# A mixture of 32 experts in plain float32, by quarters of 32 slots on column tiles, with 20 weight tiles in flight, in a fused diffusion block

## The chip, the cores and the metric

One core of one Trainium2 chip runs the whole block as one program. TensorE (PE) multiplies matrices, VectorE (DVE) and ScalarE (ACT) work elementwise, GpSimd (POOL) issues the indirect transfers, SyncE (SP) issues most of the others, and 16 DMA engines move the data between the chip's memory and the core. The metric is the device time of one execution in microseconds (us); smaller is better.

## The reference

A token-mixing sub-layer (a state-space branch and a convolution branch) comes first and isn't touched by the change. The second sub-layer is a mixture of experts over 512 tokens of 1024 channels: each token goes to 2 of 32 experts, and each expert is a SwiGLU with a hidden width of 256. A last normalisation follows.

```python
def hier_moe(h, w_rg, b_rg, w_rx, b_rx, w_gate, w_up, w_down):
    ...
    expert_id = g_idx * EXPERTS_PER_GROUP + top_idx
    gate = jnp.sum(jax.nn.one_hot(expert_id, N_EXPERTS, dtype=jnp.float32) * weights[..., None], axis=1)
    gate = gate.astype(h.dtype)
    out = jnp.zeros_like(h)
    for e in range(N_EXPERTS):
        act = jax.nn.silu(h @ w_gate[e]) * (h @ w_up[e])
        out = out + gate[:, e:e + 1] * (act @ w_down[e])
    return out
...
            x = x + gt2 * out.reshape(x.shape)
...
    return rmsnorm(x, g_final)
```

One expert has three matrices of 256 Ki float32 numbers, 1 MB each; all 32 have 96 such matrices, 100.7 MB. With the inputs of this case, 20 experts have at most 32 tokens, 8 have 33 to 64, 2 have 65 to 96 and 2 have more (up to 128); so cut into quarters of 32 slots, the 32 experts fill 20 + 16 + 6 + 8 = 50 quarters. The last expert fills one.

## The kernel before

The span up to about 550 us is the token mixing, the routing and its tables. Then comes the expert loop, iterations `e` = 0 to 32, with the instruction order of PE, ACT and DVE written out by hand (`tc.manual_schedule`), and a last part that adds everything up.

**Slots.** Each expert has 128 slots. `gather_e` fetches the rows of an expert's tokens into one of two buffers `xg` by an indirect transfer (line 1325), two iterations ahead. `tile_x` transposes them on PE (line 1337, eight 128x128 transposes) into `st`, as a rounded high part and a low remainder, since the matmuls run in the faster but coarser format float32r.

**Weights.** They arrive as thirds of an expert, 1 MB each, in 13 tiles that `eraw` hands out in turn: two thirds hold half of gate and up each, one holds down. `load_p(m)` issues third `m` on SP's queue. ACT and DVE split every third into a high and a low part (`unit_hi` line 1297, `unit_lo` line 1302, `unit_d_hi`, `unit_d_lo` lines 1312 and 1316).

**Products.** `tile_gu` makes 24 matmuls of 128x512 per expert (lines 1349 to 1351: high by high, low by high, high by low), always over all 128 slots; `tile_act` applies SwiGLU, `tile_at` transposes the result (line 1362), `tile_down` makes 12 matmuls (lines 1372 to 1375), `tile_y` copies them to `y` on ACT, and `scatter_e` writes the rows used with one indirect transfer to `ybuf` in memory (line 1329); branches on POOL alone choose its size. The results of the last two experts (`DIRECT`) don't go through memory: `last_y` splits them and `last_out` multiplies them with a one-hot matrix.

**Last part.** `last_loads` brings the residual stream `x1` (2 MB, twice 1 MB) and the last scale `gfin`, `last_rows` reads each token's two rows of `ybuf`. `last_add0` and `last_add1` weigh and add them on ACT, DVE and POOL, `last_out` adds the matmuls of the last two experts, squares and takes the root, `last_norm` scales and writes each block of 128 tokens out.

PE's order in an iteration is: half of gate and up of `e`, transposes of the activations of `e-1`, transposes of `x` for `e+1`, down of `e-1`, second half of gate and up of `e`.

Of the kernel before, what the change touches and what calls it, by code (L numbers as in the profile page):

```python
# [26 lines left out]
def hybrid_kernel(  # L27
# [952 lines left out]

    def eraw(name):
# [8 lines left out]
        if j < 11:  # L990
            return modp.tile([128, 2048], F32, tag=("ch", "cl")[j - 9], name=name)
        if j == 11:
            er2[0] = xp.tile([128, 4096], F32, tag="x16", name=name)
        return er2[0][:, 2048 * (j - 11):2048 * (j - 11) + 2048]

    def part_load(gate, up, down, h, q=SY):

        t = eraw("eraw")
        if h < 2:
            t = t.rearrange("p (a k n) -> p a k n", a=2, k=4)  # L1000
            for a, src in enumerate((gate, up)):
                q.dma_start(out=t[:, a], in_=src[512 * h:512 * h + 512].rearrange("(p k) n -> p k n", k=4))
        else:
            t = t.rearrange("p (k n) -> p k n", k=2)
            q.dma_start(out=t, in_=down.rearrange("(p k) n -> p k n", k=2))
        return t
# [3 lines left out]
    def load_p(m, *a):  # L1010
        if m < 3 * 32:
            e = m // 3
            eraws.setdefault(e, []).append(part_load(w_exp_gate[0, e], w_exp_up[0, e], w_exp_down[0, e], m % 3, *a))
# [211 lines left out]
    for m in range(7, 9):  # L1225
        load_p(m)
    NXG = 2
    gt2 = mo.tile([128, D], F32, name="gt2", tag="gt2", bufs=1)
    SY.dma_start(out=gt2, in_=adr[6:8].rearrange("(o n) d -> o (n d)", o=1).to_broadcast([128, D]))
    xgs = [mo.tile([128, D], F32, name=f"xg{j}", tag=f"xg{j}", bufs=1) for j in range(NXG)]  # L1230
# [18 lines left out]
    def indices(pt, p, n, name):  # L1249
# [10 lines left out]
        V.tensor_tensor(ix[:, 0], em[:, 0], em[:, 1], op=ALU.add)  # L1260
        return ix

    pt = ps_tp("ptab")
# [26 lines left out]
    def gu_views(r, q, u):  # L1290
        src = r[q // 2][:, :, 2 * (q % 2):2 * (q % 2) + 2, :].rearrange("p a k n -> p k a n")
        return [t.rearrange("p k (a n) -> p k a n", a=2) for t in u] + [src]
# [7 lines left out]
    def unit_lo(r, q, u, keep=False):  # L1300
        hi, lo, src = gu_views(r, q, u)
        i = V.tensor_tensor(lo, src, hi.bitcast(F32), op=ALU.subtract)  # L1302
        if keep:
            tc.keep_in_program_order(i)
        return u

    def unit_gu(r, q):
        return unit_lo(r, q, unit_hi(r, q))

    def unit_d_hi(r, q):  # L1310
        u = [mo.tile([128, 1024], F32R, tag=t, name="e" + t, bufs=2) for t in ("dh", "dl")]
        S.activation(u[0], r[2][:, q, :], AF.Copy)  # L1312
        return u

    def unit_d_lo(r, q, u, keep=False):
        i = V.tensor_tensor(u[1], r[2][:, q, :], u[0].bitcast(F32), op=ALU.subtract)  # L1316
        if keep:
            tc.keep_in_program_order(i)
        return u

    def unit_d(r, q):
        return unit_d_lo(r, q, unit_d_hi(r, q))

# [8 lines left out]
    def tile_x(xg, st, h):  # L1332

        pt = ps_tp("pxt").rearrange("p (k s) -> p k s", k=4)
        for k in range(4):

            T.transpose(pt[:, k, :], xg[:, 512 * h + k:512 * h + 512:4], ident)  # L1337
        sh_ = st[:, 4 * h:4 * h + 4]
        S.activation(sh_[:, :, 0, :], pt, AF.Copy)  # L1339
        V.tensor_tensor(sh_[:, :, 1, :], pt, sh_.bitcast(F32)[:, :, 0, :], op=ALU.subtract)  # L1340

    def new_st():
        return mo.tile([128, KD, 2, 128], F32R, tag="st", name="st")

    def tile_gu(pg, st, unit, q):
        w_h, w_l = unit
        for k2 in range(2):
            k = 2 * q + k2
            T.matmul(pg, lhsT=st[:, k, 0, :], rhs=w_h[:, k2, :], start=(k == 0), stop=False)  # L1349
            T.matmul(pg, lhsT=st[:, k, 1, :], rhs=w_h[:, k2, :], start=False, stop=False)  # L1350
            T.matmul(pg, lhsT=st[:, k, 0, :], rhs=w_l[:, k2, :], start=False, stop=(k == KD - 1))  # L1351

    def tile_act(pg):
        sg = mo.tile([128, 256], F32, tag="sge", name="sge", bufs=1)
        S.activation(sg, pg[:, 0:256], AF.Silu)
        V.tensor_tensor(sg, pg[:, 256:512], sg, op=ALU.mult)
        return sg

    def tile_at(sg):
        pa = ps_s5("pat")[:, 0:256].rearrange("p (k s) -> p k s", k=2)  # L1360
        for k in range(2):
            T.transpose(pa[:, k, :], sg[:, k:256:2], ident)
        at = mo.tile([128, 2, 2, 128], F32R, tag="at", name="at", bufs=1)
        S.activation(at[:, :, 0, :], pa, AF.Copy)  # L1364
        V.tensor_tensor(at[:, :, 1, :], pa, at.bitcast(F32)[:, :, 0, :], op=ALU.subtract)
        return at

    def tile_down(pd, at, unit, k):
        w_h, w_l = unit
# [336 lines left out]
```

## Time and profile before

| what | value |
|---|---|
| median of 3 runs | 911.4 us (910.17 to 912.75) |
| profiled execution, its own time | 909.51 us |
| span of the profiled execution | 907.8 us |
| mean granted clock of TensorE | 0.943 |
| PE busy | 778.0 us (86%) |
| DVE busy | 677.7 us (75%) |
| ACT busy | 543.7 us (60%) |
| POOL busy | 375.9 us (41%) |
| mean DMA rate over the span | 224 GB/s |

Busy times overlap, so they don't add up. The span is what the profiler recorded from the first to the last instruction; 1.7 us lie around it in the execution's own time. Busy shares are means over stages that have different limits; the windows of the trace tell them apart.

### The profile page before, as it was taken

The numbers are of one execution on the slowest core, as the hardware profiler recorded it, in microseconds if no ns is written. First come the engines' busy times: TensorE is split into PE (matmuls) and PEld (weight loads), VectorE is DVE, ScalarE is ACT, GpSimd is POOL, SyncE is SP. The second block draws the span as 40 slices with busy tenths as digits, with TensorE's granted clock in tenths as the row PEclk, the third lists the DMA queues.
The fourth block names the chain that finished last, engine by engine and source line by source line (L and its number), as shares of the span: only waits on it lengthen the run. The fifth ranks groups of instructions, "written<-read, shape, count | busy, mean of one in ns | idle before, by whom it ended". The sixth has DMA issues, their size and how long they took to land.

```text
span 907.8 us, 14079 instructions
## 1 busy us (share of the span) xinstructions
PE 778.0 (86%) x5094; PEld 602.4 (66%) x5094; DVE 677.7 (75%) x914; ACT 543.7 (60%) x839; POOL 375.9 (41%) x291
## 2 busy tenths in 40 slices
PE   3598957988878977979999976999999999999972
PEld 0376845656556765736788755788888888888751
DVE  4948473473599778637874596999999999999867
ACT  4433512435365756538432435989888898898752
POOL 4657434534477696712400221233323332333443
PEclk9988987999989998989999987999999999999976
DMA  8925951232146464468857346989999998988222
GB/s 307 254 66 168 224 188 53 72 122 71 39 143 192 132 183 162 142 233 310 287 205 296 116 184 228 393 336 340 365 367 372 375 387 327 354 307 307 80 118 92
DMA packets 89988, 201.88 MB, mean 222 GB/s; under 512 B 12558, under 2 KB 42320, under 8 KB 85810
## 3 DMA queue, kind: packets, MB, share of 16 engines
q1 hardware_dynamic: 82658, 180.00, 56.5%
q0 software_dynamic: 4832, 12.44, 3.9%
q10 hardware_dynamic: 2416, 8.44, 3.5%
q8 instruction: 40, 0.66, 0.3%
q14 instruction: 42, 0.34, 0.1%
HBM read 180.16 MB, written 22.76 MB: 224 GB/s over the span
## 4 chain that ended last, share of the span: by engine, by line
PE 53%; DVE 14%; issue 9%; DMA 9%; POOL 8%; ACT 4%; SPq 3%; ACTq 0%; POOLq 0%; DVEq 0%
PE peg L1351 6%; PE peg L1349 6%; PE peg L1350 6%; DMA wa<-in_w_ada_dram 4%; PE cp L804 3%; PE ped L1372 3%; PE pxt L1337 3%; PE ped L1373 3%; PE ped L1375 3%; POOL adacc L98 2%; PE po L1192 2%; PE po L1191 2%; PE po L1190 2%; DVE so L681 1%; DVE st L95 1%
## 5 line engine op out<-in xcount | busy, mean ns | idle before, releaser
L1302 DVE TENSOR_TENSOR ewwl<-eraw,ewwh 128x1024 fp32r<-128x1024 f32 x96 | 120.2, 1253 | 7.3 <-PE pxt L1337 4.0
L1297 ACT ACTIVATE ewwh<-eraw 128x1024 fp32r<-128x1024 f32 x96 | 101.9, 1063 | 5.8 <-DMA eraw<-in_w_exp_gate_dram 3.6
L1325 POOL DMA_INDIRECT xg<-h2d,tb x32 | 49.1, 1536 | 110.9 <-PE ped L1372 87.2
L1329 POOL DMA_INDIRECT ybuf<-ye,tb x30 | 42.6, 1421 | 94.0 <-ACT ye L1380 92.9
L1316 DVE TENSOR_TENSOR edl<-eraw,edh 128x1024 fp32r<-128x1024 f32 x64 | 75.5, 1221 | 5.8 <-ACT edh L1312 5.7
L396 PE MATMUL zp<-hh,zuwh 128*128 128x512 f32 x192 | 78.1, 407 | 0.0
L1349 PE MATMUL peg<-ewwh,st 128*128 128x512 f32 x192 | 77.4, 403 | 0.0
L1350 PE MATMUL peg<-ewwh,st 128*128 128x512 f32 x192 | 77.0, 401 | 0.0
L1351 PE MATMUL peg<-ewwl,st 128*128 128x512 f32 x192 | 76.7, 400 | 0.0
L398 PE MATMUL zp<-hh,zuwl 128*128 128x512 f32 x192 | 76.3, 398 | 0.4 <-POOL zuwl L752 0.2
L397 PE MATMUL zp<-hl,zuwh 128*128 128x512 f32 x192 | 75.9, 395 | 0.0
L1312 ACT ACTIVATE edh<-eraw 128x1024 fp32r<-128x1024 f32 x64 | 67.8, 1060 | 10.2 <-PE ped L1375 10.1
L98 POOL TENSOR_TENSOR adacc<-adacc,wa 128x512 f32<-128x512 f32 x30 | 46.2, 1540 | 41.4 <-ACT wa L854 39.0
L1372 PE MATMUL ped<-edh,at 128*128 128x512 f32 x128 | 53.2, 416 | 1.2 <-ACT at L1364 1.2
L1373 PE MATMUL ped<-edl,at 128*128 128x512 f32 x128 | 50.2, 392 | 0.0
L808 ACT ACTIVATE cpt<-cp 128x512 f32<-128x512 f32 x16 | 8.3, 602 | 61.3 <-PE cp L804 49.7
L396 PEld LDWEIGHTS zp<-hh,zuwh 128*128 128x128 f32 x192 | 36.9, 192 | 11.6 <-issue 4.4
L398 PEld LDWEIGHTS zp<-hh,zuwl 128*128 128x128 f32 x192 | 36.6, 191 | 9.5 <-POOL zuwl L752 1.6
L1351 PEld LDWEIGHTS peg<-ewwl,st 128*128 128x128 f32 x192 | 36.7, 191 | 9.1
L1350 PEld LDWEIGHTS peg<-ewwh,st 128*128 128x128 f32 x192 | 36.4, 190 | 8.9 <-DVE st L1340 0.4
L1349 PEld LDWEIGHTS peg<-ewwh,st 128*128 128x128 f32 x192 | 36.5, 190 | 8.6 <-ACT st L1339 0.3
L397 PEld LDWEIGHTS zp<-hl,zuwh 128*128 128x128 f32 x192 | 36.8, 192 | 7.2
(491 smaller groups left out, 2207.7 us busy)
## 6 DMA issues: line engine op xcount, KB each, us to landing
eraw<-in_w_exp_down_dram SPq DMA_DIRECT2D x31, 1024.0 KB
eraw<-in_w_exp_gate_dram SPq DMA_DIRECT2D x61, 512.0 KB
eraw<-in_w_exp_up_dram SPq DMA_DIRECT2D x61, 512.0 KB
wa<-in_w_ada_dram SPq DMA_DIRECT2D x32, 512.0 KB
zr<-in_w_in_dram SPq DMA_DIRECT2D x12, 1024.0 KB
wa<-in_w_ada_dram SPq DMA_DIRECT2D x8, 1024.0 KB
ybuf<-zero ACTq DMA_DIRECT2D x4, 1024.0 KB
gd<-sg SPq DMA_DIRECT2D x16, 256.0 KB
```

What stands on the lines that cost most here:

```text
L396: T.matmul(acc, lhsT=wh, rhs=ah, start=start, stop=False)
L397: T.matmul(acc, lhsT=wh, rhs=al, start=False, stop=False)
L398: T.matmul(acc, lhsT=wl, rhs=ah, start=False, stop=stop)
L1297: S.activation(hi, src, AF.Copy)
L1302: i = V.tensor_tensor(lo, src, hi.bitcast(F32), op=ALU.subtract)
L1312: S.activation(u[0], r[2][:, q, :], AF.Copy)
L1316: i = V.tensor_tensor(u[1], r[2][:, q, :], u[0].bitcast(F32), op=ALU.subtract)
L1349: T.matmul(pg, lhsT=st[:, k, 0, :], rhs=w_h[:, k2, :], start=(k == 0), stop=False)
L1350: T.matmul(pg, lhsT=st[:, k, 1, :], rhs=w_h[:, k2, :], start=False, stop=False)
L1351: T.matmul(pg, lhsT=st[:, k, 0, :], rhs=w_l[:, k2, :], start=False, stop=(k == KD - 1))
L1372: T.matmul(pd[h], lhsT=at[:, k, 0, :], rhs=w_h[:, hs[h]], start=(k == 0), stop=False)
L1373: T.matmul(pd[h], lhsT=at[:, k, 0, :], rhs=w_l[:, hs[h]], start=False, stop=False)
```

## The change

Six edits come together.

1. The split into high and low parts is gone, with its ACT and DVE instructions. Weights and slots stay plain float32, and so do the matmuls.
2. Each expert's 128 slots are cut into quarters `a` of 32. `tile_gu` and `tile_down` run per quarter: the 32 slots are the stationary operand, on one of four 32-column tiles of the array (the output's partitions `Q[c]`), and the four tiles take four parts of the output's columns. `quarters` wraps quarters 1 to 3 in nested branches on the expert's size, on PE (for the matmuls) and on POOL (for the scatters); `load_wide` reads the size into a PE register. `scatter_q` writes one quarter by one indirect transfer in pieces of 256 numbers (1 KB), since the output's four column parts now lie on different partitions.
3. Weights in flight: `NER` = 20 thirds instead of 13. A third is now one whole matrix (gate, up or down), 8 KB on each partition. Three more tiles come from `mo`, four more thirds from pairs of tiles of `wp` (`PIECES`) that were used for the split weights of the token mixing. The order of the ring changes with it: thirds 7 to 12 are issued when the token mixing's pool is closed, 13 to 16 on ACT's queue, 17 and 18 on SP's, the others at the end of each iteration.
4. `tile_y` moves from ACT to DVE and multiplies by the sub-layer's gate `gt2q` there, which the last part did before.
5. Tables of the scatter get four quarters (`ixq`, 16 small matmuls and one DVE instruction, once).
6. The last part adds in PSUM: `last_x` puts the residual into PSUM accumulators `fin` by an identity matmul, `last_own` adds the last two experts, `last_mix` adds the weighed rows by an identity matmul, `last_sum` squares, `last_root` and `last_norm` finish. POOL takes no part in it any more.

The core of the diff:

```diff
-        j = erc[0] % 13
+        while erc[0] % NER in PIECES:
+            erc[0] += 1
+        j = erc[0] % NER
...
-    def unit_hi(r, q):
-        u = wpair(q, [2, 512], "ew")
-        hi, lo, src = gu_views(r, q, u)
-        S.activation(hi, src, AF.Copy)
-        return u
...
-            T.matmul(pg, lhsT=st[:, k, 0, :], rhs=w_h[:, k2, :], start=(k == 0), stop=False)
-            T.matmul(pg, lhsT=st[:, k, 1, :], rhs=w_h[:, k2, :], start=False, stop=False)
-            T.matmul(pg, lhsT=st[:, k, 0, :], rhs=w_l[:, k2, :], start=False, stop=(k == KD - 1))
+    def tile_gu(pg, st, r, a):
+        for k in range(KD):
+            for c in range(4):
+                src = r[c // 2][k // 4][:, 256 * (k % 4) + c % 2:256 * (k % 4) + 256:2]
+                T.matmul(pg[Q[c], 128 * a:128 * a + 128], lhsT=st[:, k, Q[a]], rhs=src, start=(k == 0), stop=(k == KD - 1), skip_group_check=True)
...
+    def tile_down(pd, at, r, a):
         for k in range(2):
+            for c in range(4):
+                T.matmul(pd[a // 2][Q[c], 256 * (a % 2):256 * (a % 2) + 256], lhsT=at[:, 64 * a + 32 * k:64 * a + 32 * k + 32], rhs=r[2][k][:, 256 * c:256 * c + 256],
+                         start=(k == 0), stop=(k == 1), skip_group_check=True)
...
+    def scatter_q(e, a, y):
+        return G.indirect_dma_start(out=ybuf.rearrange("r (c n) -> (r c) n", c=4), out_offset=bass.IndirectOffsetOnAxis(ap=ixq[:, a, e:e + 1], axis=0),
+                                    in_=y[:, 256 * a:256 * a + 256], in_offset=None, bounds_check=8 * L - 1, oob_is_err=False)
+
+    def quarters(size_, f):
+
+        r = [f(0)]
+        with tc.If(size_ > SIZES.index(32)):
+            r.append(f(1))
+            with tc.If(size_ > SIZES.index(64)):
+                r.append(f(2))
+                with tc.If(size_ > SIZES.index(96)):
+                    r.append(f(3))
+        return r
...
+        for a in range(4):
+            for c in range(4):
+                V.tensor_tensor(y[Q[a], 256 * c:256 * c + 256], pd[a // 2][Q[c], 256 * (a % 2):256 * (a % 2) + 256], gt2q[Q[c]], op=ALU.mult)
...
+    def last_mix(i):
         y = yrs[i][:, 0]
+        S.activation(y, y, AF.Copy, scale=pw[:, i, 0:1])
         V.scalar_tensor_tensor(y, yrs[i][:, 1], pw[:, i, 1:2], y, op0=ALU.mult, op1=ALU.add)
...
+        for h in range(2):
+            T.matmul(fin[i][h], lhsT=ident, rhs=y[:, 512 * h:512 * h + 512], start=False, stop=True, skip_group_check=True)
...
+                quarters(wide[e], lambda a: tile_gu(pgs[e % 2], st[e], eraws[e], a))
+            load_wide(e + 1)
+            if e == NE:
+                last_x(0)
             if e > 0:
                 at = tile_at(sg)
+            if e == NE:
+                fin[1], fin[2] = pgs, [ps_tp(f"fin2{i}") for i in range(2)]
+                last_x(1)
+                last_x(2)
...
+                quarters(wide[e - 1], lambda a: tile_down(pd, at, eraws[e - 1], a))
...
+            for m in range(3 * e + 19, 3 * e + 22):
+                load_p(m)
```

How the instructions stand now, in three places. The first is PE's order between two experts. Before, it reads like this (`peg` is the sum of gate and up, `pat` the transposed activations, `pxt` the transposed slots, `ped` the sum of down):

```order
L1349 MATMUL peg<-ewwh,st 128x512
L1350 MATMUL peg<-ewwh,st 128x512
L1351 MATMUL peg<-ewwl,st 128x512
L1362 MATMUL pat<-ident,sge 128x128 x2
L1337 MATMUL pxt<-ident,xg_4857 128x128 x8
L1372 MATMUL ped_7128<-edh,at 128x512
L1391 UNCONDITIONAL_BRANCH
L1373 MATMUL ped_7128<-edl,at 128x512
L1372 MATMUL ped_7129<-edh,at 128x512
L1373 MATMUL ped_7129<-edl,at 128x512
L1375 MATMUL ped_7128<-edh,at 128x512
```

In the changed kernel the same place on PE reads (line 1409 is the branch past quarters 1 to 3, lines 1411 and 1413 are the inner ones):

```order
L1348 MATMUL peg_5173<-eraw,st 32x128 x32
L1409 COMPARE_AND_BRANCH
L1348 MATMUL peg_5173<-eraw,st 32x128 x32
L1411 COMPARE_AND_BRANCH
L1348 MATMUL peg_5173<-eraw,st 32x128 x32
L1413 COMPARE_AND_BRANCH
L1348 MATMUL peg_5173<-eraw,st 32x128 x32
L1413 UNCONDITIONAL_BRANCH x2
L1411 UNCONDITIONAL_BRANCH
L1409 UNCONDITIONAL_BRANCH
L1617 TENSOR_LOAD size
L1359 MATMUL pat<-ident,sge 128x64 x4
```

Gate and up stand in one piece ahead of the transposes, the weights come straight from the loaded tiles (`eraw`), and three of the four quarters are behind branches; the eight transposes of `pxt` and the quarters of `ped`, branched over in the same way, follow.

The second place is SP's queue around the start of the expert loop. Before, up to the load of the gate `gt`:

```order
L1183 DMA wo<-in_w_o_dram 128x4x512 x2
L1005 DMA eraw<-in_w_exp_down_dram 128x2048
L1175 DMA xr<-in_x_dram 128x4x1024
L1002 DMA eraw<-in_w_exp_gate_dram 128x1024
L1002 DMA eraw<-in_w_exp_up_dram 128x1024
L1183 DMA wo<-in_w_o_dram 128x4x512 x2
L1002 DMA eraw<-in_w_exp_gate_dram 128x1024
L1002 DMA eraw<-in_w_exp_up_dram 128x1024
L1005 DMA eraw<-in_w_exp_down_dram 128x2048
L1002 DMA eraw<-in_w_exp_gate_dram 128x1024
L1002 DMA eraw<-in_w_exp_up_dram 128x1024
L1005 DMA eraw<-in_w_exp_down_dram 128x2048
```

In the changed kernel, up to the same load:

```order
L1195 DMA wo<-in_w_o_dram 128x4x512 x2
L1017 DMA eraw<-in_w_exp_down_dram 128x2048
L1187 DMA xr<-in_x_dram 128x4x1024
L1017 DMA eraw<-in_w_exp_gate_dram 128x2048
L1195 DMA wo<-in_w_o_dram 128x4x512 x2
L1017 DMA eraw<-in_w_exp_up_dram 128x2048
L1017 DMA eraw<-in_w_exp_down_dram 128x2048
L1014 DMA eraw<-in_w_exp_gate_dram 128x1024 x2
L1014 DMA eraw<-in_w_exp_up_dram 128x1024 x2
L1014 DMA eraw<-in_w_exp_down_dram 128x1024 x2
L1014 DMA eraw<-in_w_exp_gate_dram 128x1024 x2
L1242 DMA gt_4865<-adr 128x1024
```

The four thirds of line 1014 (two transfers each) now stand ahead of `gt`; the rows of before above are followed by `gt` at once.

The third place is ACT at the very end, after the last copy of `at`. Before (`yr` are the rows read back, `x` the residual, `ssf` the sums of squares):

```order
L1647 ACTIVATE rs_3713<-rs_3713 128x4
L1559 ACTIVATE yr<-yr,pw 128x1024 x4
L1538 ACTIVATE ypwh<-ye 128x512 x2
L1579 ACTIVATE yr,ssf<-x_9409 128x1024
L1580 ACTIVATE ssf<-ssf,eps 128x1
L1579 ACTIVATE yr,ssf<-x_9409 128x1024
L1580 ACTIVATE ssf<-ssf,eps 128x1
L1586 ACTIVATE x_9409<-x_9409,ssf 128x1024
```

In the changed kernel (`yp` is the split result of the last expert, `fin` the accumulators in PSUM; the second block of tokens uses the banks of `peg`):

```order
L1559 ACTIVATE yp<-ye,gs 128x1024
L1675 ACT_TABLE_LOAD
L1675 ACTIVATE rs_3713<-rs_3713 128x4
L1591 ACTIVATE yr<-yr,pw 128x1024
L1598 ACTIVATE yr,ssf<-fin_5177 128x512
L1598 ACTIVATE yr,ssf<-fin_5178 128x512
L1591 ACTIVATE yr<-yr,pw 128x1024
L1602 ACTIVATE ssf<-ssf,eps 128x1
L1598 ACTIVATE yr,ssf<-peg_5173 128x512
L1598 ACTIVATE yr,ssf<-peg_5174 128x512
```

The four weighings (line 1559 before, 1591 now) no longer stand together ahead of the rest: from the second block on, each stands behind the squares of the block before it.

## Rows read from the trace of the kernel before

**Rows 1.** The page's first line.

```profile
span 907.8 us, 14079 instructions
```

**Rows 2.** Windows of the span: busy time by engine, granted clock, DMA share, GB/s.

```profile
405.00:420.00 15.00, 13.43 (x50) 8.87 (x50) 11.24 (x12) 11.42 (x14) 1.46 (x1) 1.00 0.94 376
532.00:547.00 15.00, 7.88 (x48) 6.14 (x46) 14.16 (x57) 4.02 (x7) 3.44 (x5) 0.69 0.72 254
547.00:570.00 23.00, 16.68 (x74) 13.57 (x75) 14.88 (x37) 14.64 (x19) 5.44 (x5) 0.76 0.66 239
570.00:600.00 30.00, 28.44 (x136) 23.21 (x136) 27.66 (x42) 27.42 (x39) 7.96 (x6) 1.00 0.93 351
600.00:750.00 150.00, 150.00 (x719) 124.60 (x718) 138.97 (x158) 133.74 (x189) 47.65 (x32) 1.00 1.00 369
750.00:830.00 80.00, 80.00 (x389) 66.70 (x388) 73.55 (x84) 70.68 (x101) 25.05 (x17) 1.00 0.91 338
830.00:836.00 6.00, 6.00 (x28) 4.84 (x27) 5.89 (x8) 5.73 (x9) 1.88 (x2) 1.00 0.88 322
836.00:842.00 6.00, 6.00 (x32) 5.09 (x31) 5.38 (x7) 4.93 (x7) 4.08 (x3) 1.00 0.01 4
```

**Rows 3.** Timeline of PE over one expert: start, time from first start to last end.

```profile
702.76 0.39 PE L1362 MATMUL pat<-ident,sge 128*128 128x128 f32 x2
...
702.99 1.12 PE L1337 MATMUL pxt<-ident,xg 128*128 128x128 f32 x8
...
712.34 0.39 PE L1362 MATMUL pat<-ident,sge 128*128 128x128 f32 x2
```

**Rows 4.** Timeline of SP's queue: the last issue of expert weights.

```profile
818.03 0.33 SPq L1005 DMA_DIRECT2D eraw<-in_w_exp_down_dram  x1
```

**Rows 5.** Timeline of PE: plain float32 matmuls, and the first expert matmul.

```profile
74.95 1.07 PE L259 MATMUL pm<-wa,condz 128*32 128x256 f32 x16
...
75.95 0.44 PE L576 MATMUL pxc<-ident,ctok 128*128 128x128 f32 x2
...
399.16 3.60 PE L1023 MATMUL pmu<-cacc,ones 128*128 128x512 f32 x8
...
555.45 0.80 PE L1349 MATMUL peg<-ewwh,st 128*128 128x512 f32 x1
```

**Rows 6.** Lines 1418 and 1417 on PE's queue: duration ns min/median/max, starts.

```profile
L1418 PEldq COMPARE_BRANCH  x1: 228/228/228, 549.6 to 549.6; - x1
...
L1418 PEldq EVENT_SEMAPHORE  x1: 51/51/51, 549.8 to 549.8; - x1
...
L1417 PEldq TENSOR_LOAD <-ngen x1: 492/492/492, 549.0 to 549.0; - x1
```

**Rows 7.** A window of the convolution's matmuls, line 804 alone.

```profile
167.00:175.30 8.30, 8.26 (x248) 5.32 (x248) 1.00 0.39 129
```

**Rows 8.** Lines 1329 (scatter) and 1325 (gather): duration on POOL; landing.

```profile
L1329 POOL DMA_INDIRECT ybuf<-ye,tb x30: 1341/1370/1928, 573.0 to 853.7; - x30
...
DMA to landing us min/median/max: 2.6/7.1/9.4
```

**Rows 9.** Timeline of PE after the last expert.

```profile
877.84 0.49 PE L1577 MATMUL pf<-ypwh,st 128*128 128x512 f32 x1 [2.89 <-ACT ypwh L1538]
...
885.22 0.63 PE L1577 MATMUL pf<-ypwh,st 128*128 128x512 f32 x1
...
886.02 0.40 PE L1577 MATMUL pf<-ypwh,st 128*128 128x512 f32 x1
```

**Rows 10.** Line 1356 by its tile, and timelines of ACT and DVE at the end.

```profile
L1356 DVE TENSOR_TENSOR sge<-peg,sge x32: 411/418/425, 565.5 to 869.9; 128x256 f32<-128x256 f32 x32
...
883.67 1.06 ACT L1579 ACTIVATE yr<-x 128x1024 f32<-128x1024 f32 x1 [5.22 <-DVE x L1578]
...
873.98 2.48 DVE L1563 SCALAR_TENSOR_TENSOR yr<-yr,pw 128x1024 f32<-128x1024 f32 x2 [2.13 <-ACT yr L1559]
...
902.77 1.29 DVE L1589 SCALAR_TENSOR_TENSOR x<-x,ssf,gfin 128x1024 f32<-128x1024 f32 x1
```

More of the change, by code (lines that the diff above doesn't have):

```diff
@@ L1224, in hybrid_kernel @@
     mz2 = ctx.enter_context(tc.tile_pool(name="mz2", bufs=1, side="right", reuse_waits="tile"))
-    for m in range(7, 9):
+    mo_.append(mo)
+    for m in range(7, 13):
         load_p(m)
@@ L1556, in last_rows, with last_x, last_own @@
             xis.append(x1s[i // 2][:, i % 2])
-    def last_add0(i):
-        S.activation(yrs[i][:, 0], yrs[i][:, 0], AF.Copy, scale=pw[:, i, 0:1])
-    def last_add1(i):
+    def last_x(i):
+        for h in range(2):
+            T.matmul(fin[i][h], lhsT=ident, rhs=xis[i][:, 512 * h:512 * h + 512], start=True, stop=False, skip_group_check=True)
+    def last_own(j, parts):
+        for i in range(NT):
+            for r_ in parts:
+                for h in range(2):
+                    T.matmul(fin[i][h], lhsT=last["oh"][:, 512 * j + 128 * i:512 * j + 128 * i + 128], rhs=r_[:, 512 * h:512 * h + 512], start=False, stop=False, skip_group_check=True)
@@ L1572, in last_out, with last_sum, last_root, last_norm @@
+    def last_sum(i):
+        for h in range(2):
+            S.activation(yrs[i][:, 1, 512 * h:512 * h + 512], fin[i][h], AF.Square, accum_out=ssf[:, h, i:i + 1])
+    def last_root(i):
+        V.tensor_tensor(ssf[:, 2, i:i + 1], ssf[:, 0, i:i + 1], ssf[:, 1, i:i + 1], op=ALU.add)
+        S.activation(ssf[:, 3, i:i + 1], ssf[:, 2, i:i + 1], AF.Sqrt, bias=eps, scale=1.0 / D)
+    def last_norm(i):
+        V.reciprocal(ssf[:, 3, i:i + 1], ssf[:, 3, i:i + 1])
+        xi = xis[i]
         for h in range(2):
@@ L1592, in hybrid_kernel, with load_wide @@
     MAN = {EN.PE, EN.Activation, EN.DVE}
-    ug, ud_, st, pgs = {}, {}, {}, {}
+    st, wide = {}, {}
+    def load_wide(e):
+        if e < NE:
+            wide[e] = nc.values_load(size[0:1, e:e + 1], engines=[EN.PE], min_val=0, max_val=len(SIZES) - 1, skip_runtime_bounds_check_because=BYC)
+    pgs = [ps_s5(f"peg{i}") for i in range(2)]
+    pd = [ps_mm(f"ped{i}") for i in range(2)]
+    fin[0] = [ps_mm(f"fin{i}") for i in range(2)]
     with tc.manual_schedule(engines=MAN):
+        for t in pgs + pd:
+            V.memset(t, 0.0)
+        load_wide(0)
@@ L1666, in hybrid_kernel @@
                 last_rows()
-        for i in range(NT):
-            if i > 1:
-                last_add1(i)
-            last_out(i)
+        S.activation(rs2, rs2, AF.Sqrt)
+        fin[3] = pd
+        last_x(3)
+        for j in range(2):
+            last_own(j, last["y", j])
+        for i in range(NT + 1):
+            if i < NT:
+                last_mix(i)
+            if i > 0:
+                last_root(i - 1)
+            if i < NT:
+                last_sum(i)
             if i > 0:
                 last_norm(i - 1)
-        last_norm(NT - 1)
 _INS = ['x', 'c', 'ctx', 'c_ctx', 'w_ada', 'b_ada', 'g_mix', 'g_ffn', 'w_in',
```

247 lines of the change are left out of this document (91 added, 156 removed).

## Prediction

> **What bounds the kernel now.** I read the page's first line for the span, 907.8 us [rows 1], and then the windows, because the shares of the whole span mix stages. In the expert loop the window from 600 to 750 us shows PE busy 150.00 of 150.00 us and, in the same row, a DMA share of 1.00 at 369 GB/s [rows 2]. So two things are at their limit at once. The timeline of PE gives the period of an expert: from 702.76 to 712.34, 9.58 us [rows 3]. The reader is to see that less work on PE alone buys little: the loop then waits for weights. The sum must therefore be made three times, for PE, for the chain of gather and scatter, and for the weights; the latest sets the end of the loop, and the last part follows.
>
> **PE's own work after the change.** A plain float32 matmul runs as two instructions: line 1023 shows eight of 128x512 in 3.60 us, 0.45 us each [rows 5]. On 32-column tiles line 259 shows 16 instructions of 256 columns begun and left behind between 74.95 and 75.95 [rows 5]: four sets of four, 0.25 us a set at most. Were the four tiles one behind another, 16 x 0.225 (half of 0.45) = 3.6 us would be needed; so the tiles run side by side. From line 1023 a set of 256 columns costs 0.225 us. A quarter of gate and up is 8 x 2 sets of 128 columns: 16 x 0.11 to 0.125 = 1.8 to 2.0 us; a quarter of down is 2 x 2 sets of 256: 0.9 to 1.0 us. I take 2.7 us a quarter; 50 quarters are 135 us. Per expert come eight transposes, 1.12 us [rows 3], four transposes of 64 columns at about 0.45 (between the 0.39 us of the present pair and twice that), one read of the size, 0.49 us, and branches: the one branch on PE's queue took 0.228 + 0.051 us [rows 6], two of them in each iteration make 0.56. That is 2.6 x 32 = 84 us. The sum is 219 us; from the first expert matmul at 555.45 [rows 5] PE would be through at about **775 us**, if nothing else held it.
>
> **Gather and scatter.** A gather into a buffer can start when the transposes of the expert two before have read it, and it stands on POOL among the scatters. Once round is two experts: landing 7.1 us (median, 2.6 to 9.4), a scatter 1.37 us on POOL [rows 8], transposes 1.1, down 0.9, the product of two halves on DVE about 1.4 (estimated from 0.418 us for 256 columns, [rows 10]), 0.5 for handing over: 12.4, or 6.2 us an expert. Each of the 18 quarters above one an expert adds about 1.15 (2.7 on PE, or one more scatter of 1.37, shared by two experts). 32 x 6.2 + 18 x 1.15 = 219 us: about 775 us too.
>
> **The weights.** The last third was issued at 818.03 [rows 4]. The DMA engines were quiet from 836 on (share 0.01), and busy for 0.88 of the six us ahead, so until 835.3 [rows 2]. The last things moved were x1 and the scale, 2.6 MB, 7 us at 369 GB/s; so the last third landed at about 829. What can more tiles in flight give? They fill the times in which the DMA engines had nothing: 15 x 0.28, 23 x 0.34, 30 x 0.07 and 80 x 0.09 in the windows from 532 on [rows 2], 4.2 + 7.8 + 2.1 + 7.2 = 21.3 us. 829 - 21.3 = 807.7. Pieces of 8 KB instead of 4 KB a partition and fewer stalls may help the rate; 376 GB/s at a share of 0.94 in 405 to 420, weights with no gathers, is 400 GB/s at full share [rows 2]. From 570 on that would turn 238 us into 220, a landing at 790. The other bound is the present 829, no gain. I take 805, near the row of the stage itself. So weights come last, 30 us behind the other two, and PE waits for them.
>
> **The last part.** After 805 these stand one behind another. The 1 MB of x1 that follows: 2.8 us, to 808. `last_x(0)` stands ahead of the last transposes of activations on PE, so all behind it wait for x1: four instructions of 0.45, 1.8; transposes 0.5; `last_x` 1 and 2, 3.6; down of expert 31, 0.9: 815. Sixteen products on DVE of 256 columns at about 0.4 [rows 10]: 6.5, to 821.5. `last_x(3)` needs the same banks; then 32 matmuls of `last_own`. In before PE, after 2.89 us without work, took 0.63 us for these until 885.22 and 0.40 from 886.02 on [rows 9]; starts lay 0.43 and 0.235 apart. PE has idled for six here, so I count 3.6 for `last_x(3)`, 12 matmuls at 0.43 and 20 at 0.235: 835. `last_mix(0)` 1.8 and two squares with their sums, 1.4 (half of 1.06 each [rows 10], and 0.2 to read a sum): 838. Then three rounds, each in series, because ACT's next weighing stands behind the squares: weighing 1.06, sum on DVE 1.24 (2.48 for two), identity matmuls 1.8 at the full clock and 3.5 at the lower, squares 1.4, handing over 0.4: 5.9 to 7.6. PE idles about 4 us between, more than the 2.89 above, so I take 7.1 and end at 859.5. Root and reciprocal 0.6, two halves of 0.65 [rows 10], and from the end of the last instruction of DVE (902.77 + 1.29 = 904.06) to the end of the span it takes 3.7 us: **865**. The profiled execution had 909.51 beside its span of 907.8, and is 1.9 under the median of 911.4: 865 + 1.7 + 1.9 = 868.6; since most pieces of the last part were rounded up, I say **867 us**.
>
> The splits on ACT and DVE go at no gain of their own (both lay beside PE). Products on DVE, 1.4 us an expert, are hidden by a wait for weights. If weights stopped being last, they would lie in the chain of gather and scatter, where they are counted. The tables for quarters (16 small matmuls and an instruction, once) I cost at nothing, since the first gather, 7.1 us, starts from the other table and covers them; uncovered they would be about 2 us.
>
> [...] Where code runs straight, PE shows no pause: 248 matmuls of line 804 kept it busy for 8.26 of 8.30 us [rows 7]. After the change, 20 of 32 experts jump over three quarters of gate and up, some 100 matmuls. The one branch on PE's queue, with the wait behind it, took 0.28 us [rows 6], and that is what the sum counts. [...] No run here shows a jump that far. [...]
>
> **Rivals.**
> - *Jumps stall PE.* Bounds for one iteration's stalls: nothing beyond the 0.56 us counted, and 7.1 us (a small transfer from memory, as the gather's landing). PE has 805 - 775 = 30 us to spare, 0.9 us an expert; the last part takes 62 us after it. At 1.5 us an expert PE ends at 823 and the result is about 885. It ends on the other side, **slower**, when PE's end comes 44 us after 805: (849 - 775) / 32 = 2.3 us an expert. At 3.2 us the result is about 940. For: the target is far and not reached by straight code. Against: the branch row's 0.28 us, though that branch may be a near one.
> - *The clock falls in the loop*, since PE will wait for weights there. The window from 547 to 570, with PE busy for 16.68 of 23 us, has a granted clock of 0.76; the one from 405 to 420, with 13.43 of 15, has 1.00 [rows 2]. At 0.76 PE's 219 us become 288 and end at 844, for about 906; but then PE waits no more and looks like the second row. It matters below 219 / 250 = 0.88. I expect at most some ten us of it, 867 to 880.
> - *The DMA engines go faster*, near 400 GB/s: weights land at 790, PE and gathers end at 775, and the result is 837 to 852.
> - *Small pieces slow the stream.* Weights now flow at 3.15 MB in 9.58 us, 328 GB/s; of the other 41 about half are scatters, 5.5 % of 369. They will be pieces of 1 KB instead of 4 KB a row. If they took twice their time, the weights from 570 on would land 13 us later: 880.
> - *Column tiles don't overlap* when the weights are read at every second number: 135 us of quarters become 540, a result over 1200. Line 259's row speaks against it.
>
> **How the numbers follow.** Weights last, as summed: 0.44, with 855 to 880 as its own range. Faster DMA: 0.14. Moderate stalls of jumps, or a fallen clock, 870 to 905: 0.20. Slow pieces: 0.09. Stalls above the turning point: 0.09. Tiles not side by side: 0.02; others 0.02. The time is that of the first. The range of 834 to 900 leaves out the last cases, the end of the moderate one and some of the fast one. About 0.3 %, 2.7 us, is what a measurement of this kernel can tell from no change: faster 0.87, same 0.02, slower 0.11.
>
> **What would show it.** Right: in the windows of the loop a DMA share of 1.00 with PE well under its full time, PE's waits ended by transfers of `eraw`, quarters of gate and up of 1.8 to 2.0 us, the last third near 805, three rounds of 6 to 7.5 us at the end. Wrong: PE without work and with no transfer behind it just after a branch (jumps), a DMA share under 0.95 in the loop (PE or gathers last), fewer GB/s at full share (pieces).

## The result and the profile after

The changed kernel takes 1063.71 us (median of 4 runs, 1054.67 to 1070.75) where the kernel before takes 910.78: 1.165 times as long, 95% interval 1.155 to 1.175. The forecast was 867 us and faster. The profiled execution (span 1069.0 us) is the longest of the four, 1.5% above the shortest and left out of the ratio; what follows is far larger than that.

The page after, its span, PE's busy time and the DMA queue that the page calls instruction:

```profile
span 1069.0 us, 19679 instructions
...
PE 762.2 (71%) x8070; PEld 553.0 (52%) x8070; DVE 473.4 (44%) x747; ACT 322.1 (30%) x559; POOL 345.9 (32%) x310
...
q8 instruction: 115, 1.88, 0.7%
```

The last of these rows read like this before:

```profile
q8 instruction: 40, 0.66, 0.3%
```

Against the rows of before, PE is busy for less of the span (71% against the 86% of the table), and has 8070 matmul instructions against 5094, since a quarter on column tiles takes many small ones. The instruction queue moved 1.88 MB in 115 packets of 16 KB, where before it moved 0.66 MB in 40; it is the queue to keep in mind. Before, PE executed 5094 matmuls and as many weight loads, with one conditional branch on its queue [rows 6]; if this queue carries PE's code alone, 0.66 MB for 10188 instructions are 65 bytes each (an estimate), and the 384 instructions of three quarters of gate and up 25 KB.

The windows of the loop and of the last part (columns as in [rows 2]):

```profile
600.00:750.00 150.00, 94.33 (x1612) 68.17 (x1610) 29.62 (x44) 16.81 (x32) 26.63 (x27) 0.77 0.69 247
750.00:900.00 150.00, 85.22 (x1422) 61.78 (x1423) 26.95 (x40) 15.91 (x31) 27.20 (x28) 0.77 0.66 240
1000.00:1069.00 69.00, 39.43 (x130) 19.97 (x130) 28.83 (x57) 16.10 (x31) 0.00 (x0) 0.75 0.23 92
```

In [rows 2] the loop had PE at 150.00 of 150.00 us and a DMA share of 1.00. Now PE is at 94.33, at a granted clock of 0.77, and the DMA share is 0.69: neither limit of before is reached, and neither are the weights that the prediction put last. Something else makes PE wait. The timeline of PE over an expert with one quarter says where:

```profile
651.53 1.97 PE L1329 MATMUL pxt<-ident,xg 128*128 128x128 f32 x8
653.44 1.94 PE L1367 MATMUL ped<-eraw,at 128*32 128x256 f32 x16
656.57 2.57 PE L1348 MATMUL peg<-eraw,st 128*32 128x128 f32 x64 [1.20 <-PEq L1409]
666.25 0.66 PE L1359 MATMUL pat<-ident,sge 64*128 64x64 f32 x4 [7.11 <-PEq L1409]
```

The reader is to see the last row: gate and up of one quarter begin at 656.57 and take 2.57 us, and then PE does nothing for 7.11 us until `pat`, released by PE's own sequencer at line 1409, the branch past quarters 1 to 3. The view of waits adds these up over the loop (us in total, times, longest):

```profile
PEld pat L1359 <- PEq L1409: 110.4, 19, 7.4
PEld peg L1348 <- issue: 49.5, 53, 2.4
PEld pat L1359 <- PEq L1411: 30.0, 8, 6.8
...
PEld pat L1359 <- PEq L1413: 3.1, 2, 1.9
```

110.4 us in 19 waits, 5.8 us each, behind line 1409 (three quarters jumped over), 30.0 in 8 behind line 1411 (two quarters), 3.1 in 2 behind line 1413 (one). The branches themselves, by line:

```profile
L1409 PEldq COMPARE_BRANCH  x64: 65/233/6861, 566.6 to 1021.5; - x64
```
```profile
L1411 PEldq COMPARE_BRANCH  x40: 65/187/6542, 674.8 to 1004.0; - x40
```
```profile
L1413 PEldq COMPARE_BRANCH  x16: 65/186/437, 676.6 to 807.9; - x16
```

So one branch instruction lasts up to 6.86 us over three quarters, up to 6.54 over two and never more than 0.44 over one. A quarter of gate and up is 64 matmuls and 64 weight loads. The branch of [rows 6], with its 0.228 us, was as cheap as the last kind.

What the long ones wait for stands in the trace too. Of the 120 records of these three lines, 28 last longer than 1 us: 27 behind quarters of gate and up, one behind quarters of down. Laid beside the packets of the instruction queue, each of the 28 has a packet that lands while the branch lasts, and the branch ends 1.34 to 1.53 us after that landing; of the 92 short ones, four have a landing within them. In the window of the branch in the timeline above, 658.72 to 665.52 us, the queue's row is this:

```profile
q8 instruction: 2, 0.03, 2.4%
```

So I read a long branch as a wait for code, by the name of the queue and by these times; what a packet holds, the trace doesn't say. From the branch's start to the start of the packet ahead of its end 3.15 us pass (median, at most 4.5), the packet takes about 1.0 us, and 1.4 us follow. The distance sorts the long from the short, and not strictly: of the 28 skips of two or three quarters of gate and up 27 were long, of the skips of one quarter none; one of the eight skips of two quarters took 0.43 us, without a packet, and one skip of three quarters of down, 48 matmuls and 48 weight loads, took 2.62 us, with one.

### The profile page after: what moved, and what is told of

Read it like the earlier page. It is cut to its first block, busy times and chain, and to the rows that moved or that the text cites. A ratio compares the mean times of both kernels' runs of the same rounds, so it can differ in the third digit from the quotient of the medians.

```text
span 1069.0 us, 19679 instructions
## 1 busy us (share of the span) xinstructions
PE 762.2 (71%) x8070; PEld 553.0 (52%) x8070; DVE 473.4 (44%) x747; ACT 322.1 (30%) x559; POOL 345.9 (32%) x310
## 3 DMA queue, kind: packets, MB, share of 16 engines
q8 instruction: 115, 1.88, 0.7%
## 5 line engine op out<-in xcount | busy, mean ns | idle before, releaser
L1348 PE MATMUL peg<-eraw,st 128*32 128x128 f32 x3200 | 117.5, 293 | 25.8 <-PEq L1409 9.8
L1348 PEld LDWEIGHTS peg<-eraw,st 128*32 128x32 f32 x3200 | 101.9, 115 | 53.4 <-issue 49.5
L1359 PEld LDWEIGHTS pat<-ident,sge 64*128 64x128 f32 x128 | 14.5, 190 | 155.0 <-PEq L1409 110.4
L1403 POOL DMA_INDIRECT ybuf<-ye,ixq x47 | 46.7, 994 | 130.2 <-DMA ybuf<-ye,ixq 57.8
L1367 PE MATMUL ped<-eraw,at 128*32 128x256 f32 x800 | 76.6, 535 | 1.7 <-issue 1.7
L1329 PE MATMUL pxt<-ident,xg 128*128 128x128 f32 x256 | 59.9, 407 | 14.0 <-DMA xg<-h2d,tb 6.9
L1377 DVE TENSOR_TENSOR ye<-ped,gt2q 128x512 f32<-128x512 f32 x60 | 39.0, 687 | 56.6 <-PE ped L1367 27.7
L1329 PEld LDWEIGHTS pxt<-ident,xg 128*128 128x128 f32 x256 | 47.4, 216 | 18.5 <-issue 14.9
L1367 PEld LDWEIGHTS ped<-eraw,at 128*32 128x32 f32 x800 | 30.2, 145 | 35.8 <-issue 30.0
L98 POOL TENSOR_TENSOR vb<-vta,vtb 128x512 f32<-128x512 f32 x16 | 22.3, 1393 | 30.0 <-PE pv L533 19.1
L752 DVE TENSOR_TENSOR zuwl<-zr,zuwh 128x1024 fp32r<-128x1024 f32 x16 | 28.4, 1775 | 5.7 <-ACT zuwh L751 5.6
```

What stands on the lines that cost most here:

```text
L98: G.tensor_tensor(o, a, b, op=op)
L752: (G if t in ZPOOL else V).tensor_tensor(zu[t][1], raw, zu[t][0].bitcast(F32), op=ALU.subtract)
L1329: T.transpose(pt[:, k, :], xg[:, 4 * h + k:D:8], ident)
L1348: T.matmul(pg[Q[c], 128 * a:128 * a + 128], lhsT=st[:, k, Q[a]], rhs=src, start=(k == 0), stop=(k == KD - 1), skip_group_check=True)
L1359: T.transpose(pa[:, 64 * a:64 * a + 64], sg[64:128, 128 * a:128 * a + 128], ident[64:128, 64:128])
L1367: T.matmul(pd[a // 2][Q[c], 256 * (a % 2):256 * (a % 2) + 256], lhsT=at[:, 64 * a + 32 * k:64 * a + 32 * k + 32], rhs=r[2][k][:, 256 * c:2 ...
```

## The experiments

Four questions: are the jumps the cause, how does their cost depend on traffic and distance, what is behind them, and is there a version that beats both kernels? All times are medians, or of one run where that is said; before stood at 908.4 to 912.3 beside them.

**No branch on PE (e1_static).**

```diff
-                quarters(wide[e], lambda a: tile_gu(pgs[e % 2], st[e], eraws[e], a))
-            load_wide(e + 1)
+                for a in range(NQ[e]):
+                    tile_gu(pgs[e % 2], st[e], eraws[e], a)
```

`tile_down` likewise; `NQ` is the list of quarters for these inputs, 50 in all.

> The changed kernel with each expert's number of quarters written into the program (for these inputs), so that PE has no branch and no read of a size; the matmuls executed, POOL's branches, the loads and the last part are the same. Theory J (PE stalls after a jump over the quarters left out, and the low clock in the loop is the consequence): the 5.8 us behind the branch vanish, the weights bound the loop, and the time is 860 to 890 us. Theory C (PE has too little work, its clock falls and doubles its matmuls, and the wait at the branch is only where that shows): the work and the idle share stay, granted clock in the loop under 0.85, over 980 us. Theory D (scatter in 1 KB pieces or the ring of 20 slows the transfers): DMA share stays near 0.7 at under 260 GB/s, over 1000 us.

Measured: 910.15 us, ratio to before 0.9986 (0.9955 to 1.0017). The same matmuls without the jumps and the reads of the size save 153 us, so theory J holds and C and D fall: the DMA share is 0.92 with the same 1 KB pieces, and the granted clock is 0.86 where it was 0.77. The instruction queue moves 64 packets in place of 115. But 910 is 20 us over the upper end expected. In the loop PE is still far from full, though no longer for the weights alone:

```profile
600.00:750.00 150.00, 99.93 (x2188) 80.71 (x2178) 31.94 (x48) 18.86 (x36) 35.52 (x37) 0.86 0.92 352
```
```profile
POOL ybuf L1403 <- DMA ybuf<-ye,ixq: 73.9, 13, 9.4
```
```profile
DVE ye L1377 <- DMA ybuf<-ye,ixq: 60.6, 7, 15.9
```
```profile
PE pat L1359 <- DVE sge L1353: 62.6, 18, 15.9
```

POOL waits 73.9 us, 13 times, for a scatter to land before it issues the next one. These are the quarters of one expert: the kernel declares scatters of different experts independent, but not those of one. The second and third rows show how the wait reaches PE: the late scatters hold the two buffers `ye`, DVE waits for one of them, its part of the SwiGLU (`sge`) stands behind that, and PE waits for `sge`.

**The scatters of one expert set free, without and with PE's branches (e5_static_free, e6_free).**

```diff
-        for i_ in ins:
-            for p_ in scattered:
+        for n_, i_ in enumerate(ins):
+            for p_ in scattered + ins[:n_]:
                 tc.declare_no_dep(...)
```

> e1_static (no branches on PE) with the waits between the scatters of one expert's quarters taken away: they write different rows, and are now declared so, as those of different experts already are. Theory S (the second cause is that an extra quarter's scatter waits until the one before has landed, 6 to 7 us, and holds POOL's queue and the next gather; 73.9 us of such waits stand in the trace of e1_static): the loop ends 30 to 40 us earlier, bound by weights at about 810, and the time is 865 to 885 us. Rival (the 73.9 us lie beside the wait for weights, DMA share is 0.92 in that loop already): 900 to 910 us.

> The changed kernel, branches on PE kept, with the same waits between scatters taken away. Theory J first: PE's stalls behind the branches set the loop and hide most of these waits, so 1040 to 1060 us. Theory S alone: 1000 us or less.

Measured: e5_static_free 879.88 us, 0.9648 (0.961 to 0.9685); e6_free 1059.09 us in one run. So the waits cost 30 us, once the jumps are gone, and nothing that shows beside them. Without both, the loop is near what the prediction described:

```profile
600.00:750.00 150.00, 132.90 (x2719) 101.69 (x2720) 47.09 (x70) 28.25 (x54) 47.06 (x49) 0.98 1.02 388
```

DMA share 1.02 at 388 GB/s, PE 132.90 of 150 us busy at a clock of 0.98. The two runs differ in PE's branches and reads alone, so the stretch from the first to the last matmul of gate and up tells what these cost (e6_free first, then e5_static_free):

```profile
559.33:984.62 425.29, 254.89 (x4320) 185.26 (x4320) 83.64 (x134) 52.33 (x96) 80.76 (x84) 0.79 0.63 227
```
```profile
563.14:811.42 248.28, 212.90 (x4319) 164.80 (x4320) 83.68 (x134) 52.34 (x96) 82.38 (x85) 0.97 1.01 384
```

The stretch is 177 us longer with branches. PE is idle for 170.4 us of it in place of 35.4, and busy 42 us longer with the same matmuls at the lower granted clock.

**The same jumps without the weights' traffic (e2_noloads).**

```diff
-        if m < 3 * 32:
+        if m < 18:
...
+        for e in range(6, NE):
+            eraws[e] = eraws[2 + (e - 2) % 4]
```

> The changed kernel without the loads of experts 6 to 31: they multiply with the weights of experts 2 to 5, so the output is not the reference's and 82 MB are not moved. All branches of PE stay. Theory J1 (the stall is the fetch of code behind the weights' traffic in the same DMA engines): the wait at the branch falls from 5.8 us to 2 to 3 us, and the time to 930 to 980 us. Theory J2 (the stall has a fixed length): it stays at 5 to 7 us and the time is 1020 to 1065 us. Theory C or D: no wait for weights can remain, so the time falls to under 900 us.

Measured: 966.45 us in one run. With a DMA share of about 0.1 in the loop the wait shrinks, but doesn't go:

```profile
PEld pat L1359 <- PEq L1409: 63.9, 19, 4.3
...
PEld pat L1359 <- PEq L1411: 18.3, 8, 3.3
```

63.9 us in 19 waits are 3.4 us each, against 5.8. So of a far jump's price some 3.4 us are there with nearly idle DMA engines, and 2.4 come with the weights' traffic. J1 has the time right and is a little low on what is left of the wait (2 to 3 us). The packets say where the 2.4 us go: in all 26 long branches of this run one lands, 1.29 to 1.57 us ahead of the branch's end, but it starts 0.93 us after the branch does (median), not 3.15. C and D forecast under 900 us and are out.

**A far jump added to the kernel before (e4_jump).**

```diff
+                load_wide(e)
+                with tc.If(wide[e] > SIZES.index(96)):
+                    jk = ps_tp("junk")
+                    for i in range(96):
+                        T.matmul(jk[0:32, 0:128], lhsT=ident[:, 0:32], rhs=ident, start=True, stop=True)
```

> The kernel before with one branch more in each expert, behind gate and up: PE reads the expert's size and jumps over 96 small matmuls (24 KB of code, as three quarters of gate and up have), which only the two largest experts execute. Reading the size adds 0.5 us an expert and the executed matmuls some 20 us in all: about 945 us if a jump costs no more than the 0.28 us of the branch on PE's queue. Theory J: 30 jumps at 4 to 7 us more, 1065 to 1155 us, with PE idle behind the branch and a DMA share under 0.8 in the loop.

Measured: 986.4 us in one run, 75 more than before, between the two. The branches do take long, yet PE waits little:

```profile
L1661 PEldq COMPARE_BRANCH  x34: 70/3743/6295, 563.3 to 940.9; - x34
...
  PE peg L1349: 15.1, 10
```
```profile
652.08 21.15 PE L1664 MATMUL junk<-ident 128*32 128x128 f32 x192
```
```profile
705.57 0.19 PEld L1351 LDWEIGHTS peg<-ew_l,st 128*128 128x128 f32 x1
706.31 0.19 PEld L1349 LDWEIGHTS peg<-ewwh,st 128*128 128x128 f32 x1 [0.56 <-issue]
```

The median branch lasts 3743 ns, 25 of the 34 records last 3.0 us or longer (110 us together), and `peg` waited for it 10 times, 15.1 us in all. Most of the 75 us is something else: the added matmuls, which two experts execute, take 21 us for each of them, 42 where 20 were expected. The rest, some 18 us, has no cause shown here. At the branch of 702.3 PE goes on for 3.5 us with the matmuls ahead of it, and its weight loads pause for 0.56 us only (706.31): some fifteen matmuls of 0.235 us cover 3.5 us of this jump. In the changed kernel a matmul of gate and up is worth some 0.03 us (64 in 2.0 to 2.6), PE's last one starts only 0.15 to 0.9 us after the long branch behind them does, and nearly the whole branch shows. My expectation left that cover out.

**Hints (e3_hint, e9_early).**

```diff
+            tc.mark_branch_hint_location(label, hint=size_ > SIZES.index(32), engines=[EN.PE])
         r = [f(0)]
-        with tc.If(size_ > SIZES.index(32)):
+        with tc.If(size_ > SIZES.index(32), label=label):
```

In e9_early the hint for gate and up stands behind `load_wide(e + 1)`, and the scatters are free as in e6_free.

> The changed kernel with a prefetch hint for each of PE's branches over quarters, placed one quarter of matmuls ahead of the branch and set by the expert's size. Theory J: where the target is fetched ahead, the wait at the branch falls to under 2.5 us and the time to 880 to 960 us; if the fetch takes longer than the quarter of matmuls ahead (2 to 2.7 us), about half of the wait stays. Theory C or D: no change, 1050 to 1070 us.

> e6_free (branches on PE kept, waits between scatters of an expert gone) with the hint for gate and up's first branch given as soon as PE has read that expert's size: ahead of the transposes and of down of the expert before, instead of right ahead of the quarter. That is 6 us or more ahead of the branch, where e3_hint gave it some 2 us ahead and the wait only went from 5.8 to 5.4 us. If the hint starts the fetch and only came late: the wait falls under 1.5 us and the time to 890 to 930 us. If a hint is lost when another branch or the next block of straight code comes between, or does nothing for this kind of branch: the wait stays at 4.5 us or more and the time at 1030 to 1060 us.

Measured: e3_hint 1061.93 us, 1.1661 (1.1565 to 1.1757), no gain; e9_early 1032.08 us in one run, 27 less than e6_free. The waits of `pat` behind the first branch of gate and up (line 1417 in e3_hint, the first fence; line 1412 in e9_early, the second):

```profile
PEld pat L1359 <- PEq L1417: 101.7, 19, 7.6
```
```profile
PEld pat L1359 <- PEq L1412: 67.6, 18, 6.8
PEld pat L1359 <- issue: 47.0, 9, 9.5
```

5.4 us each with the hint a quarter ahead. With the early one 67.6 in 18 are 3.8 us, while `pat` waits another 47.0 us in 9 for an issue; together 4.2 us each. Neither end of my expectation holds: in this one run an early hint goes with shorter waits, and doesn't make the jump cheap. The packets fit: the one ahead of the branch's end still starts behind the branch's own start in 26 of the 32 long branches of e3_hint and in 24 of the 28 of e9_early, as in 27 of the 28 of the changed kernel. Why it starts no sooner with the hint was not settled.

**Two halves in place of four quarters (e7_halves).**

```diff
-    Q = [slice(32 * c, 32 * c + 32) for c in range(4)]
+    Q = [slice(64 * c, 64 * c + 64) for c in range(2)]
...
-            for c in range(4):
-                src = r[c // 2][k // 4][:, 256 * (k % 4) + c % 2:256 * (k % 4) + 256:2]
-                T.matmul(pg[Q[c], 128 * a:128 * a + 128], ...)
+            for c in range(2):
+                src = r[c][k // 4][:, 256 * (k % 4):256 * (k % 4) + 256]
+                T.matmul(pg[Q[c], 256 * a:256 * a + 256], ...)
```

Down, the products, the tables and the scatter follow with two column parts of 512.

> The changed kernel with two halves of 64 slots on two 64-column tiles in place of four quarters: 64 matmul instructions and as many weight loads for a half of gate and up become 16 matmuls as written (64 instructions in all, 4 KB of code, against 24 KB that three quarters leave out), 28 of 32 experts leave out one half, 4 run both; scatter pieces are 2 KB. PE computes more slots (36 halves of 64 against 50 quarters of 32, 44 % more matmul time). Theory J (the distance of the jump decides): the wait behind the branch falls under 1.5 us and the time to 875 to 910 us. If any taken branch costs the 5.8 us, whatever its distance: 1040 us or more.

Measured: 903.53 us, 0.9913 (0.9877 to 0.995): 160 us below the changed kernel, and 0.5 to 1.2% below the one before, with more matmul work than the quarters. The skip is now 32 matmuls and 32 weight loads, and no branch of line 1409 is long:

```profile
L1409 PEldq COMPARE_BRANCH  x72: 65/208/344, 563.4 to 855.7; - x72
```
```profile
600.00:750.00 150.00, 137.37 (x986) 86.32 (x984) 43.18 (x64) 24.40 (x47) 35.19 (x36) 1.00 0.96 362
```

At most 344 ns where the quarters had 6861, and no packet of instructions lands within any of the 72. PE is busy for 137.37 of 150 us at the full clock.

**The last part in another order (e8_halves_tail, e12_static_tail) and two orders more (e10_halves_order).**

```diff
-        for i in range(NT + 1):
-            if i < NT:
-                last_mix(i)
+        last_own(0, 3)
+        for i in range(NT):
+            last_mix(i)
+        for i in range(NT + 1):
+            if i < NT:
+                last_own(1, i)
...
+                last_weigh(0)
+                last_weigh(1)
+                last["y", 1] = last_y(pd, 1)
```

> e7_halves with the waits between scatters of one expert taken away and the last part put in another order: the rows read back are weighed and summed for all four blocks before the last expert's result is split, all identity matmuls stand ahead of the last expert's own, and last_x comes behind the last down. In e1_static the last part took 63 us from the last gate and up, of which the three rounds of weighing, summing, identity matmuls and squares took about 20 us and the wait for sixteen products of the expert before 7 us. Expected: 20 to 25 us less than e7_halves, 850 to 885 us. If the last part is bound by something else (the reading of rows after the last scatter), 5 us less or no change.

> e8_halves_tail with two orders changed: PE reads the next expert's size behind the eight transposes instead of right behind the branch (in e8_halves_tail PE idles about 0.7 us there in each expert, 0.3 of it for the read), and the activations of the last expert stand ahead of the split of the expert before, so that its down doesn't wait for it (4.4 us in e8_halves_tail). Expected: 32 x 0.3 = 10 us and 5 us less than e8_halves_tail, 875 to 885 us. If the weights bound the loop already (DMA share 0.96), only the 5 us: 887 to 891 us.

> e5_static_free (quarters without branches on PE, without the waits between scatters) with the last part in the order of e8_halves_tail. In e5_static_free the last gate and up begins to end at 811 us and 65 us follow; the new order took 9 us off the kernel with halves. Expected: 860 to 870 us, near the 867 that the prediction summed for a kernel without stalls. If the last part here waits for x1 and the rows read back, no gain: 876 to 880 us.

Measured: e8_halves_tail 894.39 us (0.9742 to 0.9841 of before), 9 less than e7_halves where 20 to 25 were expected; e10_halves_order 879.25 (0.9591 to 0.9711), 15 less again, as expected where the weights don't bound the loop; e12_static_tail 863.36 (0.947 to 0.9553), 16.5 less than e5_static_free, of which some 4 us are a faster kernel before beside it (908.44 against 912.27). Beside before, the last part of the change is a loss: from the start of the last gate-and-up matmul to the end of the span it takes 65 us in e5_static_free and 73 in the changed kernel, and 38.7 in before.

**Thirteen thirds in flight (e11_thirteen).**

```diff
-        for m in range(13, 17):
-            load_p(m, S)
-        for m in range(17, 19):
-            load_p(m)
...
-            for m in range(3 * e + 19, 3 * e + 22):
+            for m in range(3 * e + 13, 3 * e + 16):
```

> e10_halves_order with 13 thirds of weights in flight instead of 20: the ring keeps its 20 tiles, but thirds 13 to 18 aren't issued ahead of the loop, and each iteration issues the three that follow 13 ahead. The prediction gave the six or seven more tiles 21 us, by the times without transfers that they fill. If that holds where PE is near its limit too (142 of 150 us busy in e10_halves_order): the weights land late by 10 to 21 us and the time is 885 to 900 us. If PE sets the pace of e10_halves_order alone: within 3 us of it.

Measured: 873.35 us, 0.9631 (0.9584 to 0.9679), the same as e10_halves_order within the intervals. The loss expected isn't there: with PE near its limit (142.37 of 150 us busy in e10_halves_order) the tiles beyond 13 bring nothing that shows. Whether they do where weights bound the loop wasn't tried.

## Why the prediction was wrong

**The step that failed** is the price of the branches, "two of them in each iteration make 0.56". I took it from the only branch on PE's queue [rows 6], which skips the short code of a path for experts with more than 128 tokens (31 matmuls as written). In the changed kernel the far branch behind gate and up costs 5.8 us for 19 experts and 3.75 for the 8 that leave out two quarters, 143 us in all by the view of waits (110.4 + 30.0, and 3.1 for line 1413). The rival said this, with an upper bound near the longest wait (7.1 us, the landing of a gather [rows 8], against 7.4), the right place and the side on which it ends, and got 0.09 above the turning point of 2.3 us. Its price is 4.5 us an iteration here, 143 / 32, for which its own sum gives 980 us; the rest is in the next step. That a far target costs more was shown by no row of before: it was an estimate there, as its bound was. The straight code of line 804 [rows 7] that I set against it says nothing on jumps: PE was busy for 8.26 of 8.30 us there, with no branch among the matmuls. The runs show what jumps do: every long branch of the changed kernel and of e2_noloads ends 1.3 to 1.6 us after a packet of the instruction queue has landed, one quarter's skip stays at 0.44 us or less, three quarters' takes 6.0 (median), and less (3.3) when the DMA engines are nearly idle (e2_noloads).

**A second step failed with it**: I held that PE's clock can't cost much, since a PE that is late doesn't idle. Without the branches the clock was 0.98 from 600 to 750 us, with PE busy for 132.90 of 150 (e5_static_free). Here PE idles behind its own branch, however late it is, and the clock stays at 0.77. The rivals counted jumps and clock as one or the other; they come together. The two rows of e6_free and e5_static_free put them at 135 us of idle time and 42 us of longer matmuls, where the second rival had 69 for the clock alone (219 us at 0.76). The rest of the miss is small: in the changed kernel the first matmul of gate and up starts at 564.3 us in place of 555.5, and the last part, from the start of the last one, takes 73 us in place of 60.

**The chain of gather and scatter** was mis-sized: an extra quarter was priced at 1.15 us, and in e1_static 13 of the 17 extra scatters waited 5.7 us each (73.9 in all) for the one before. I had not read that the kernel declares only other experts' scatters independent. It cost 30 us in e1_static against e5_static_free, and is hidden in the changed kernel.

**Right** were the end of the weights, the matmuls and, in its total, the last part. With jumps and scatter waits gone (e5_static_free) the DMA engines are full at 388 GB/s (bounds 369 and 400), the last gate and up waits until 809.47 us for its weights, where 805 was the landing, and from its last matmul at 811.4 us the rest takes 65 us, where 60 were summed:

```profile
809.47 2.23 PE L1348 MATMUL peg<-eraw,st 128*32 128x128 f32 x60 [1.99 <-DMA eraw<-in_w_exp_up_dram]
...
826.00 0.69 PE L1359 MATMUL pat<-ident,sge 64*128 64x64 f32 x4 [7.26 <-DVE sge L1353]
```

The second row is a wait that the sum doesn't have: on DVE the last SwiGLU stands behind the sixteen products of the expert before. That 60 came near 65 without these 7.26 us is luck in part. A quarter of gate and up takes 2.0 us (e1_static: 128 matmuls, two quarters, in 3.88 us at 667.97), as summed for four column tiles side by side. The rounds at the end were summed at 7.1 us; PE's timeline of the changed kernel has them at 6.5 to 6.7:

```profile
1045.22 3.40 PE L1594 MATMUL peg<-yr,ident 128*128 128x512 f32 x4 [3.13 <-DVE yr L1592]
1051.76 3.55 PE L1594 MATMUL fin<-yr,ident 128*128 128x512 f32 x4 [3.13 <-DVE yr L1592]
1058.45 3.62 PE L1594 MATMUL ped<-yr,ident 128*128 128x512 f32 x4 [3.13 <-DVE yr L1592]
```

Each waits 3.13 us for the sum on DVE, and the four matmuls take 3.40 to 3.62 us, at a granted clock of 0.76 from 1040 us on. The small pieces slow nothing (388 GB/s at a DMA share of 1.02 in e5_static_free), which rules out that rival. More tiles in flight, 21 us in the sum, were not shown to be worth anything: e11_thirteen has a DMA share of 1.01 from 570 to 600 us and of 0.99 at 382 GB/s from 600 to 750 with 13 thirds. So the landing near 805 may have another reason than the sum gives, and be luck in part; what raised the rate from 369 GB/s was not tested by itself.

**What remains of the change's gain**: 863.36 us with straight code, which holds for these inputs alone, and 873 to 879 us with branches that skip little. Both are below 910.

## What to carry to other kernels

Price a branch by how much code it jumps over, not by the one branch that happens to be in the trace: here skipping 64 matmuls cost 0.2 to 0.4 us and skipping 192 cost 6, so fewer and larger instructions behind a branch, even with more work in them, won 160 us. Compare the instruction queue's row on the page between versions: 115 packets here, 64 without branches, 53 with halves. Look at how long the matmuls ahead of a branch go on once it has begun: some fifteen of 0.235 us hid 3.5 us of it in e4_jump, while here the last small one started 0.15 to 0.9 us after it and nearly the whole branch showed. And when work is cut into pieces that write to one place, check that their transfers don't wait for one another to land.

## What the runs showed of the hardware beyond that

A taken branch over 192 matmuls and 192 weight loads on PE lasted 2.5 to 6.9 us with the weights' traffic (20 cases, median 6.0) and 1.9 to 6.4 with the DMA engines nearly idle (median 3.3), over 128 and 128 it lasted 2.3 to 6.5 in seven cases of eight and 0.43 in one, over 64 and 64 at most 0.44. Every branch longer than 1 us in the changed kernel and in e2_noloads ended 1.3 to 1.6 us after a 16 KB packet of the instruction queue had landed; with the weights' traffic that packet started 3.15 us after the branch (median), without it 0.93. At one branch of e4_jump PE went on for 3.5 us with matmuls of 0.235 us; in the changed kernel its last small one started 0.15 to 0.9 us after the long branch behind it. The granted clock of a loop in which PE idles behind its branches stayed at 0.77 over 300 us, while the same matmuls without the branches ran at 0.98 from 600 to 750 us (e5_static_free).
